# Expert-choice search of a hybrid diffusion step: step counts summed on VectorE, fp32r one-hot products for the ninth expert

## Chip, cores and metric

One core of a Trainium2 chip runs the whole kernel. The metric is device time in microseconds (us), the median of several executions. PE is TensorE's matmul queue, DVE is VectorE, ACT is ScalarE, POOL is GpSimd, SP issues most DMAs.

## The reference

One layer of a backbone: token mixing (projections, pooling, a bidirectional recurrence, gates) and then a mixture of 16 experts, for 128 context tokens and 1024 latent tokens of width 1024. The part that matters here is the mixture:

```python
def _expert_choice_moe(h, router_w, w1, w3, w2):
    bsz, n, d = h.shape
    cap = CAPACITY_FACTOR * n // N_EXPERTS
    aff = jax.nn.softmax(jnp.einsum('bnd,de->bne', h.astype(jnp.float32), router_w.astype(jnp.float32)), axis=-1)
    gate, idx = lax.top_k(jnp.swapaxes(aff, 1, 2), cap)
    xs = jax.vmap(lambda hb, ib: hb[ib])(h, idx)
    hid = jax.nn.silu(jnp.einsum('becd,edf->becf', xs, w1)) * jnp.einsum('becd,edf->becf', xs, w3)
    out = jnp.einsum('becf,efd->becd', hid, w2) * gate[..., None].astype(h.dtype)
    y = jax.vmap(lambda ib, ob: jnp.zeros((n, d), ob.dtype).at[ib.reshape(-1)].add(ob.reshape(-1, d)))(idx, out)
    return y.astype(h.dtype)
```

Each expert takes the 128 latent tokens (`cap`) with the largest affinity to it, and 16 of the context tokens. All of it is in float32.

## The kernel before

**Experts.** Up to about 811 us the kernel mixes tokens and routes; from there to the end it runs the experts, one after the other. An expert has 24 weight chunks of 1 MB. Each is loaded to `raw`, rounded to fp32r by ACT (`hi`, L1284), and DVE writes what rounding lost as bf16 (`lo`, L1290); the load of a later chunk is issued when `lo` is done with `raw`. PE multiplies high parts with `highs` (L1475) and low parts with `lows` (L1485). Four blocks `fb`, each for w1 and w3, and in each two pairs `q` of 128 columns make the hidden values; then the down projection makes `ot` (matrices `hh`, `hb`). After each pair `sums` adds the two halves of a PSUM accumulator: ACT copies one half (L1495), DVE adds the other (L1496). The accumulators come from a pool of three, so a pair starts when the sum of the pair three places before it is done. PE, DVE and ACT each work through their own queue in the order in which the code is written (`manual_schedule`); there is no planner.

**Search.** Which tokens an expert gets is found by a search for its threshold, three bits of the float at a time. `search(e0, e1)` is a generator for the n = e1 - e0 experts of a group: search(1, 5) runs in expert 0, search(5, 10) in experts 1 to 3, search(10, 16) in experts 4 to 6. Expert 0 needs no search of its own (its list is made before it). One `next` of it stands after `sums` of nearly every pair in expert 0 and after the first pair of each block in the later ones. The latent affinities `l8` lie as 128 partitions x 8 tiles x 16 experts. One step:

- DVE makes 8 candidate thresholds (`cand`) and compares all values with 7 of them: `msk`, 128 x (7 x 8 tiles x n), bf16 ones and zeros; plane 0 is all ones and is set once.
- PE multiplies `msk` with a matrix of ones, one product per tile, eight accumulated in one PSUM tile: the counts over partitions and tiles, on every partition.
- DVE keeps the candidates that enough tokens reach (`met`, L1387) and takes the largest (`th`, L1388).

After ten steps the search marks which values lie above the threshold and which equal it (`ge`), and PE numbers the marked tokens: one product with the triangle `upto`, seven with `ones` for the tiles before, eight more to count those above. From that DVE makes the places `slo`. `list_hot` and `list_make` (L1151, L1162 to L1167) turn an expert's places into its list, and `x_fetch` gathers the tokens from DRAM by it. In expert 0 this chain feeds expert 1 at once; later ones have an expert's time.

**Context tokens.** Their expert outputs are collected in `yps`, eight experts at a time. `finish_prompt(0)` (in expert 8, the ninth) transposes them, scales them by the gate (ACT, L1599), multiplies them with a one-hot matrix `oh` and adds them to `x2p`. `finish_prompt(1)` does so at the end.

Of the kernel before, what the change touches and what calls it, by code (L numbers as in the profile page):

```python
# [8 lines left out]
F32 = mybir.dt.float32  # L9
F32R = mybir.dt.float32r  # L10
BF16 = mybir.dt.bfloat16
I32 = mybir.dt.int32
U32 = mybir.dt.uint32
AF = mybir.ActivationFunctionType
OP = mybir.AluOpType
# [4 lines left out]
P = 128  # L20
D = 1024
# [28 lines left out]
def hybrid_step_kernel(ctx: ExitStack, tc: tile.TileContext, x_prompt, x_sample, state_lru, c, c_ctx,  # L50
# [14 lines left out]
    def tp_tile():  # L65
        return tpp.tile([P, 512], F32, name="tp")
# [1300 lines left out]

    l8 = lg[:, 1:, :]
    cand = ep.tile([P, 8, E], I32, name="cand")
    msk = ep.tile([P, 8, 8, E], BF16, name="msk")  # L1370
    V.memset(msk[:, 0], 1.0)

    def search(e0, e1):

# [2 lines left out]
        for b in range(10):  # L1377
            V.tensor_tensor(cand[:, :, es], bits[:, b, :, None].to_broadcast([P, 8, n]),
                            th.bitcast(I32)[:, None, es].to_broadcast([P, 8, n]), op=OP.bitwise_or)
            V.tensor_tensor(msk[:, 1:, :, es], l8_[:, None].to_broadcast([P, 7, 8, n]),  # L1380
                            cf[:, 1:, None, :].to_broadcast([P, 7, 8, n]), op=OP.is_ge)
            yield
            t = tp_tile()
            tv = t[:, :8 * n].rearrange("p (a b) -> p a b", a=8)
            for i in range(8):
                PE.matmul(tv, ones, msk[:, :, i, es], start=i == 0, stop=i == 7)
            V.scalar_tensor_tensor(met[:, :, es], tv, float(CAP), cf, op0=OP.is_ge, op1=OP.mult)  # L1387
            V.tensor_reduce(ths, met[:, :, es].rearrange("p a b -> p b a"), axis=AX.X, op=OP.max)  # L1388

        tb = ths[:, None, :].to_broadcast([P, 8, n])  # L1390
        V.tensor_tensor(ge[:, 0, :, es], l8_, tb, op=OP.is_gt)
        V.tensor_tensor(ge[:, 1, :, es], l8_, tb, op=OP.is_equal)
        yield
        t = tp_tile()[:, :16 * n].rearrange("p (m a b) -> p m a b", m=2, a=8)
        PE.matmul(t, upto, ge[:, :, :, es], start=True, stop=False)
        for i in range(1, 8):
            PE.matmul(t[:, :, i:], ones, ge[:, :, :8 - i, es], start=False, stop=False)
        for k in range(8):
            PE.matmul(t[:, 1], ones, ge[:, 0, k, None, es].to_broadcast([P, 8, n]), start=False, stop=k == 7)
        st = stg[:, :, :, es]  # L1400
        V.tensor_tensor(st, t, ge[:, :, :, es], op=OP.mult)
        V.scalar_tensor_tensor(st[:, 1], st[:, 1], float(CAP), st[:, 1], op0=OP.is_le, op1=OP.mult)
# [183 lines left out]

    def finish_prompt(g):

        oh = ep.tile([P, P], F32R, name="oh").bitcast(F32)
        V.tensor_scalar(oh, iof, pgf[:, g:g + 1], None, op0=OP.is_equal)  # L1590
        yield
        yp, pr = yps[g], []
        for h in range(2):
            t = tp_tile()
            for k in range(4):
                PE.transpose(t[:, k * P:(k + 1) * P], yp[:, 4 * h + k, :], ident)
            pr.append(ep.tile([P, 512], F32, name=f"pr{h}", tag=("h1", "ht")[h]) if g else
                      ew.tile([P, D], F32, name="rows", bufs=2)[:, :512])
            A.activation(pr[h], t, AF.Copy, scale=pgv[:, g:g + 1])  # L1599
            if g or h:  # L1600
                yield
        ts = []
        for h in range(2):
            hs = slice(h * 512, (h + 1) * 512)
            t = tp_tile()
            PE.matmul(t, oh, pr[h], start=True, stop=True)
            if g:
                yield
            V.tensor_tensor(x2p[:, hs], x2p[:, hs], t, op=OP.add)
            if g:  # L1610
                A.activation(last["junk"][:, :512], x2p[:, hs], AF.Square, accum_out=sqe[:, 3 + h:4 + h])
                yield


    find = search(1, 5)
# [201 lines left out]
```

## Time and profile before

| | us |
|---|---|
| median of 3 runs | 2096.61 (2096.43 to 2097.95) |
| profiled execution | 2096.98 |
| its span in the trace | 2095.2 |
| PE busy | 2036.8 (97%) |
| DVE busy | 1702.2 (81%) |
| ACT busy | 1365.5 (65%) |
| raw loads of expert weights | 380 of 1 MB, 7.1 us from issue to landing (median) |

Busy times are of one profiled execution. An engine's timeline says when an instruction starts, how long it takes, and in brackets how long the engine had been idle before it and what ended that. A busy share is an average over stages with different limits, so the table is only where the reading begins.

### The profile page before, as it was taken

The page shows a single profiled execution, that of the slowest core. Times are in us where ns is not written, and L with a number is a line of the kernel's source. Part 1 is how long each engine was busy: PE and PEld are TensorE (multiplying, and loading weights), DVE is VectorE, ACT ScalarE, POOL GpSimd, SP SyncE. Part 2 cuts the span into 40 slices and gives each one's busy share as a digit, 9 for nine tenths or more (in the row PEclk, how much of TensorE's full clock was granted, in tenths as well). Part 3 has the DMA queues.
Part 4 walks back from the last instruction along what each step waited for, and adds up shares of the span by engine and source line. Part 5 has one row for each costly group of instructions (what it writes and reads, how often), then busy time and mean ns, then how long its engine had stood idle before and what let it go on. Part 6 is the DMA issues. An engine that isn't in the chain of part 4 may idle for free.

```text
span 2095.2 us, 40732 instructions
## 1 busy us (share of the span) xinstructions
PE 2036.8 (97%) x17365; PEld 1961.8 (94%) x17365; DVE 1702.2 (81%) x1907; ACT 1365.5 (65%) x1437; POOL 188.0 (9%) x327
## 2 busy tenths in 40 slices
PE   7999999999999998999999999999999999999996
PEld 4899998999999886899999999999999999999996
DVE  7788988733145467999999999998899999999997
ACT  7477676322112236777877877877777877877875
POOL 0000001010012112010011010011010010010010
PEclk9999999999999998999999999999999999999998
DMA  8143444164755239999999999999999999999996
GB/s 273 57 121 113 120 128 120 43 192 152 202 163 188 101 132 323 311 328 323 345 333 329 348 324 333 351 345 322 339 337 327 349 341 322 352 341 327 349 342 252
DMA packets 303733, 544.72 MB, mean 260 GB/s; under 512 B 16235, under 2 KB 85563, under 8 KB 303550
## 3 DMA queue, kind: packets, MB, share of 16 engines
q1 hardware_dynamic: 284074, 478.56, 65.9%
q0 software_dynamic: 15872, 53.56, 8.7%
q10 hardware_dynamic: 3604, 9.98, 1.3%
q8 instruction: 136, 2.23, 0.4%
q14 instruction: 47, 0.39, 0.1%
HBM read 501.13 MB, written 40.93 MB: 259 GB/s over the span
## 4 chain that ended last, share of the span: by engine, by line
PE 88%; DVE 7%; ACT 2%; DMA 1%; issue 1%; SPq 0%; ACTq 0%; DVEq 0%; POOLq 0%
PE ac L1475 36%; PE ac L1485 17%; PE a L196 6%; PE a L197 6%; PE a L195 6%; PE a L778 5%; DVE lo L1290 2%; PE a L1002 2%; PE a L1004 2%; PE a L1003 2%; DMA xg<-hn_d,lgi 1%; PE tp L667 1%; PE tp L1413 1%; PE tp L1040 1%; PE tp L1506 1%
## 5 line engine op out<-in xcount | busy, mean ns | idle before, releaser
L1290 DVE TENSOR_TENSOR lo<-raw,hi 128x2048 bf16<-128x2048 f32 x384 | 872.0, 2284 | 0.0
L1284 ACT CAST hi<-raw 128x2048 fp32r<-128x2048 f32 x384 | 729.7, 1912 | 7.0 <-DMA raw<-in_exp_w_dram 4.1
L1475 PE MATMUL ac<-x,hi 128*128 128x288 f32 x4096 | 585.5, 298 | 0.0
L1475 PEld LDWEIGHTS ac<-x,hi 128*128 128x128 f32 x4096 | 548.6, 188 | 1.4 <-issue 1.1
L1485 PEld LDWEIGHTS <-lo 128*128 128x128 bf16 x6144 | 382.6, 98 | 17.1 <-DVE lo L1290 0.9
L1475 PE MATMUL ac<-hh,hi 128*128 128x288 f32 x2048 | 297.3, 298 | 0.0
L1485 PE MATMUL ac<-xb,lo 128*128 128x144 bf16 x4096 | 282.7, 226 | 0.0
L1495 ACT COPY bs<-ac 128x288 f32<-128x288 f32 x320 | 127.3, 398 | 237.5 <-PE ac L1475 125.7
L1475 PEld LDWEIGHTS ac<-hh,hi 128*128 128x128 f32 x2048 | 275.4, 188 | 0.0
L197 PE MATMUL a<-hn_hi,lo 128*128 128x384 f32 x624 | 210.5, 337 | 1.9 <-DVE lo L186 1.9
L195 PE MATMUL a<-hn_hi,hi 128*128 128x384 f32 x624 | 210.4, 337 | 0.0
L196 PE MATMUL a<-hn_lo,hi 128*128 128x384 f32 x624 | 210.2, 337 | 0.0
L1485 PE MATMUL ac<-hb,lo 128*128 128x144 bf16 x2048 | 147.1, 226 | 0.6 <-DVE lo L1290 0.6
L186 DVE TENSOR_TENSOR lo<-raw,hi 128x1024 fp32r<-128x1024 f32 (+1 forms) x77 | 88.3, 1164 | 64.4 <-ACT hi L185 64.4
L1496 DVE TENSOR_TENSOR h<-ac,bs 128x288 f32<-128x288 f32 x256 | 115.6, 451 | 22.5 <-ACT bs L1495 22.5
L197 PEld LDWEIGHTS a<-hn_hi,lo 128*128 128x128 f32 x624 | 117.7, 189 | 2.3 <-DVE lo L186 2.3
L195 PEld LDWEIGHTS a<-hn_hi,hi 128*128 128x128 f32 x624 | 118.0, 189 | 0.3
L196 PEld LDWEIGHTS a<-hn_lo,hi 128*128 128x128 f32 x624 | 117.9, 189 | 0.0
L185 ACT CAST hi<-raw 128x1024 fp32r<-128x1024 f32 (+1 forms) x77 | 75.8, 1001 | 47.3 <-PE a L196 36.7
L1761 POOL TENSOR_TENSOR yps<-ot,modc 128x128 f32<-128x128 f32 x15 | 35.5, 2370 | 706.5 <-DVE ot L1496 706.5
L1496 DVE TENSOR_TENSOR ot<-ac,bs 128x288 f32<-128x288 f32 x64 | 29.1, 457 | 52.8 <-ACT bs L1495 52.8
L701 ACT ACTIVATE sg<-a 128x1152 f32<-128x1152 f32 x16 | 18.1, 1134 | 78.4 <-PE a L197 78.3
(434 smaller groups left out, 2609.6 us busy)
## 6 DMA issues: line engine op xcount, KB each, us to landing
raw<-in_exp_w_dram SPq DMA_DIRECT2D x380, 1024.0 KB, 7.1
raw<-in_w_in_dram SPq DMA_DIRECT2D x28, 512.0 KB, 4.7
raw<-in_w_mod_dram SPq DMA_DIRECT2D x28, 512.0 KB, 5.5
araw<-in_w_mod_dram SPq DMA_DIRECT2D x18, 256.0 KB, 7.1
g_d<-sg ACTq DMA_DIRECT2D x8, 576.0 KB, 3.3
yh_d<-yh POOLq DMA_DIRECT2D x8, 576.0 KB, 3.1
yl_d<-yl POOLq DMA_DIRECT2D x8, 576.0 KB, 4.6
m_d<-sg POOLq DMA_DIRECT2D x8, 576.0 KB, 4.2
```

The source lines that it names most:

```text
L185: A.copy(h, raw)
L186: V.tensor_tensor(l, raw, h.bitcast(F32), op=OP.subtract)
L195: PE.matmul(out, whi, xhi, start=first, stop=False)
L196: PE.matmul(out, whi, xlo, start=False, stop=False)
L197: PE.matmul(out, wlo, xhi, start=False, stop=last)
L778: PE.matmul(a3[:, ch, :CH], w[:, k, :], y[:, k, cs], start=n == 0 and k == 0 and w is hi, stop=n == 1 and k == KD - 1 and w is ws[-1])
L1284: A.copy(hl[n][0], raw[n])
L1290: V.tensor_tensor(lo, r, hi.bitcast(F32), op=OP.subtract)
L1475: PE.matmul(a[:, r, :2 * S], w[0][:, k, c0 + r * P:c0 + (r + 1) * P], x2(kk), start=kk == first, stop=kk == last)
L1485: PE.matmul(a[:, r, S:2 * S], w[1][:, k, c0 + r * P:c0 + (r + 1) * P], xb(kk), start=False, stop=kk == last)
L1495: A.copy(b, a[:, :, S:2 * S])
L1496: V.tensor_tensor(dst, a[:, :, :S], b, op=OP.add)
```

## The change

In each step DVE sums the comparisons over the eight tiles into `cnt` (128 x 7 x n, bf16), and PE makes one product of it with `ones`; plane 0 of the counts is eight and is set once. At a search's end DVE makes running sums over the tiles in `pre`, a view of `msk`: the first tile's entry is zero for those above and the number of all above for those equal, and seven additions give the others; PE makes two products, with `upto` and with `ones`. In `finish_prompt(0)` the scaled rows are split in an fp32r part (ACT) and the rest (DVE), and each is multiplied with the one-hot matrix in fp32r: four products where there were two in float32.

```diff
@@ -1367,8 +1367,9 @@
 
     l8 = lg[:, 1:, :]
     cand = ep.tile([P, 8, E], I32, name="cand")
-    msk = ep.tile([P, 8, 8, E], BF16, name="msk")
-    V.memset(msk[:, 0], 1.0)
+    msk = ep.tile([P, 7, 8, E], BF16, name="msk")
+    cnt = ep.tile([P, 8, E], BF16, name="cnt")
+    V.memset(cnt[:, 0], 8.0)
 
     def search(e0, e1):
 
@@ -1377,26 +1378,31 @@
         for b in range(10):
             V.tensor_tensor(cand[:, :, es], bits[:, b, :, None].to_broadcast([P, 8, n]),
                             th.bitcast(I32)[:, None, es].to_broadcast([P, 8, n]), op=OP.bitwise_or)
-            V.tensor_tensor(msk[:, 1:, :, es], l8_[:, None].to_broadcast([P, 7, 8, n]),
+            V.tensor_tensor(msk[:, :, :, es], l8_[:, None].to_broadcast([P, 7, 8, n]),
                             cf[:, 1:, None, :].to_broadcast([P, 7, 8, n]), op=OP.is_ge)
+            with nc.allow_low_precision(reason="counts of at most eight"):
+                V.tensor_reduce(cnt[:, 1:, es], msk[:, :, :, es].rearrange("p a i e -> p a e i"), axis=AX.X, op=OP.add)
             yield
             t = tp_tile()
             tv = t[:, :8 * n].rearrange("p (a b) -> p a b", a=8)
-            for i in range(8):
-                PE.matmul(tv, ones, msk[:, :, i, es], start=i == 0, stop=i == 7)
+            PE.matmul(tv, ones, cnt[:, :, es], start=True, stop=True)
             V.scalar_tensor_tensor(met[:, :, es], tv, float(CAP), cf, op0=OP.is_ge, op1=OP.mult)
             V.tensor_reduce(ths, met[:, :, es].rearrange("p a b -> p b a"), axis=AX.X, op=OP.max)
 
         tb = ths[:, None, :].to_broadcast([P, 8, n])
         V.tensor_tensor(ge[:, 0, :, es], l8_, tb, op=OP.is_gt)
         V.tensor_tensor(ge[:, 1, :, es], l8_, tb, op=OP.is_equal)
+
+        pre = msk[:, :2]
+        V.memset(pre[:, 0, 0, es], 0.0)
+        with nc.allow_low_precision(reason="counts of at most eight"):
+            V.tensor_reduce(pre[:, 1, 0, es], ge[:, 0, :, es].rearrange("p i e -> p e i"), axis=AX.X, op=OP.add)
+        for i in range(1, 8):
+            V.tensor_tensor(pre[:, :, i, es], pre[:, :, i - 1, es], ge[:, :, i - 1, es], op=OP.add)
         yield
         t = tp_tile()[:, :16 * n].rearrange("p (m a b) -> p m a b", m=2, a=8)
         PE.matmul(t, upto, ge[:, :, :, es], start=True, stop=False)
-        for i in range(1, 8):
-            PE.matmul(t[:, :, i:], ones, ge[:, :, :8 - i, es], start=False, stop=False)
-        for k in range(8):
-            PE.matmul(t[:, 1], ones, ge[:, 0, k, None, es].to_broadcast([P, 8, n]), start=False, stop=k == 7)
+        PE.matmul(t, ones, pre[:, :, :, es], start=False, stop=True)
         st = stg[:, :, :, es]
         V.tensor_tensor(st, t, ge[:, :, :, es], op=OP.mult)
         V.scalar_tensor_tensor(st[:, 1], st[:, 1], float(CAP), st[:, 1], op0=OP.is_le, op1=OP.mult)
@@ -1586,30 +1592,46 @@
 
     def finish_prompt(g):
 
-        oh = ep.tile([P, P], F32R, name="oh").bitcast(F32)
+        oh = ep.tile([P, P], F32R, name="oh")
+        if g:
+            oh = oh.bitcast(F32)
         V.tensor_scalar(oh, iof, pgf[:, g:g + 1], None, op0=OP.is_equal)
         yield
         yp, pr = yps[g], []
+        if g == 0:
+
+            for h in range(2):
+                pr.append(ew.tile([P, 2, 512], F32R, name="rows", bufs=2))
+                t = tp_tile()
+                for k in range(4):
+                    PE.transpose(t[:, k * P:(k + 1) * P], yp[:, 4 * h + k, :], ident)
+                A.activation(pr[h][:, 0], t, AF.Copy, scale=pgv[:, g:g + 1])
+                V.scalar_tensor_tensor(pr[h][:, 1], t, pgv[:, g:g + 1], pr[h][:, 0].bitcast(F32), op0=OP.mult,
+                                       op1=OP.subtract)
+            yield
+            for h in range(2):
+                hs = slice(h * 512, (h + 1) * 512)
+                t = tp_tile()
+                for a in range(2):
+                    PE.matmul(t, oh, pr[h][:, a], start=a == 0, stop=a == 1)
+                V.tensor_tensor(x2p[:, hs], x2p[:, hs], t, op=OP.add)
+            yield
+            return
         for h in range(2):
             t = tp_tile()
             for k in range(4):
                 PE.transpose(t[:, k * P:(k + 1) * P], yp[:, 4 * h + k, :], ident)
-            pr.append(ep.tile([P, 512], F32, name=f"pr{h}", tag=("h1", "ht")[h]) if g else
-                      ew.tile([P, D], F32, name="rows", bufs=2)[:, :512])
+            pr.append(ep.tile([P, 512], F32, name=f"pr{h}", tag=("h1", "ht")[h]))
             A.activation(pr[h], t, AF.Copy, scale=pgv[:, g:g + 1])
-            if g or h:
-                yield
-        ts = []
+            yield
         for h in range(2):
             hs = slice(h * 512, (h + 1) * 512)
             t = tp_tile()
             PE.matmul(t, oh, pr[h], start=True, stop=True)
-            if g:
-                yield
+            yield
             V.tensor_tensor(x2p[:, hs], x2p[:, hs], t, op=OP.add)
-            if g:
-                A.activation(last["junk"][:, :512], x2p[:, hs], AF.Square, accum_out=sqe[:, 3 + h:4 + h])
-                yield
+            A.activation(last["junk"][:, :512], x2p[:, hs], AF.Square, accum_out=sqe[:, 3 + h:4 + h])
+            yield
 
 
     find = search(1, 5)
```

How it moves instructions, at three places. DVE in expert 0, third block, a search step between two low-part splits. Before:

```order
L1496 TENSOR_TENSOR h_7400<-ac,bs 128x288
L1387 SCALAR_TENSOR_TENSOR met<-tp,cand 128x8x4
L1388 TENSOR_REDUCE th<-met 128x4
L1378 TENSOR_TENSOR cand<-bits,th 128x8x4
L1380 TENSOR_TENSOR msk<-lg,cand 128x56x4
L1290 TENSOR_TENSOR lo<-raw,hi 128x2048
```

And now:

```order
L1502 TENSOR_TENSOR h_7360<-ac,bs 128x288
L1389 SCALAR_TENSOR_TENSOR met<-tp,cand 128x8x4
L1390 TENSOR_REDUCE th<-met 128x4
L1379 TENSOR_TENSOR cand<-bits,th 128x8x4
L1381 TENSOR_TENSOR msk<-lg,cand 128x56x4
L1384 TENSOR_REDUCE cnt<-msk 128x7x4
L1290 TENSOR_TENSOR lo<-raw,hi 128x2048
```

One reduction stands between the comparison and the next split; everything else keeps its place.

DVE in expert 0, fourth block, the end of search(1, 5). Before:

```order
L1388 TENSOR_REDUCE th<-met 128x4
L1391 TENSOR_TENSOR ge<-lg,th 128x8x4
L1392 TENSOR_TENSOR ge<-lg,th 128x8x4
L1290 TENSOR_TENSOR lo<-raw,hi 128x2048
L1496 TENSOR_TENSOR h_7518<-ac,bs 128x288
```

And now:

```order
L1390 TENSOR_REDUCE th<-met 128x4
L1393 TENSOR_TENSOR ge<-lg,th 128x8x4
L1394 TENSOR_TENSOR ge<-lg,th 128x8x4
L1397 MEMSET msk 128x4
L1399 TENSOR_REDUCE msk<-ge 128x4
L1401 TENSOR_TENSOR msk<-msk,ge 128x2x4 x7
L1290 TENSOR_TENSOR lo<-raw,hi 128x2048
L1502 TENSOR_TENSOR h_7466<-ac,bs 128x288
```

Nine operations are put between the marks and the next split.

PE in expert 0, a search step among the low products (weight loads stand as rows of their own). Before, the first two of eight such pairs:

```order
L1485 LDWEIGHTS lo
L1485 MATMUL ac<-xb,lo 128x144
L1386 LDWEIGHTS ones
L1386 MATMUL tp<-msk,ones 128x32
L1386 LDWEIGHTS ones
```

And now the whole step:

```order
L1491 LDWEIGHTS lo
L1491 MATMUL ac<-xb,lo 128x144
L1388 LDWEIGHTS ones
L1388 MATMUL tp<-cnt,ones 128x32
L1491 LDWEIGHTS lo
```

Seven of the eight pairs are gone; the one that is left stands at the same place and reads `cnt`.

## Rows read from the trace of the kernel before

**Rows 1.** The page's busy times: us, share of the span, instructions.
```profile
PE 2036.8 (97%) x17365; PEld 1961.8 (94%) x17365; DVE 1702.2 (81%) x1907; ACT 1365.5 (65%) x1437; POOL 188.0 (9%) x327
```

**Rows 2.** Windows of experts 0 and 1: length, busy PE, PEld, DVE, ACT, POOL, clock, DMA.
```profile
811.00:898.70 87.70, 82.26 (x884) 79.58 (x885) 82.98 (x105) 66.66 (x64) 4.08 (x2) 0.99 0.92 322
898.70:977.10 78.40, 78.40 (x818) 77.32 (x817) 74.61 (x74) 61.95 (x60) 7.38 (x4) 1.00 0.93 325
```

**Rows 3.** Timeline of PE, expert 0: start, duration, instruction, idle before and its releaser.
```profile
851.89 0.35 PE L1386 MATMUL tp<-msk,ones 128*128 128x32 bf16 x8 [0.61 <-DVE msk L1380]
...
888.31 1.09 PE L1413 MATMUL tp<-ident,xg 128*128 128x128 f32 x8 [1.62 <-DMA xg<-hn_d,lgi]
```

**Rows 4.** Timeline of DVE, expert 0.
```profile
851.74 2.29 DVE L1290 TENSOR_TENSOR lo<-raw,hi 128x2048 bf16<-128x2048 f32 x1
...
878.77 0.16 DVE L1164 COPY lc<-tp 128x5 f32<-128x5 f32 x1
878.96 0.16 DVE L1165 SCALAR_TENSOR_TENSOR lgi<-lc 128x1 int32<-128x1 f32 x1
...
892.96 1.36 DVE L1433 TENSOR_TENSOR x<-xf,x 128x1152 fp32r<-128x1152 f32 x1 [1.83 <-ACT x L1432]
```

**Rows 5.** Groups by line and shape, reductions: count, busy us, mean ns, idle before.
```profile
L1388 DVE TENSOR_REDUCE th<-met 128x6 f32<-128x48 f32 x10 | 2.4, 236 | 0.3
L1388 DVE TENSOR_REDUCE th<-met 128x4 f32<-128x32 f32 x10 | 2.1, 210 | 0.3
L1060 DVE TENSOR_REDUCE mx<-lg 128x1 f32<-128x16 f32 x2 | 0.3, 170 | 0.6 <-ACT lg L1056 0.6
L1060 DVE TENSOR_REDUCE mx<-lg 128x5 f32<-128x80 f32 x1 | 0.2, 238 | 0.3 <-ACT lg L1056 0.3
```

**Rows 6.** Timeline of PE, a search step in expert 1 and an end in expert 3.
```profile
928.69 0.40 PE L1386 MATMUL tp<-msk,ones 128*128 128x40 bf16 x8
928.93 1.16 PE L1485 MATMUL ac<-xb,lo 128*128 128x144 bf16 x16
...
1098.76 0.22 PE L1395 MATMUL tp<-ge,upto 128*128 128x80 bf16 x1
...
1099.26 1.16 PE L1485 MATMUL ac<-xb,lo 128*128 128x144 bf16 x16
```

**Rows 7.** Timelines of DVE and PE, where the down projection begins (experts 1, 3, 5).
```profile
949.67 0.45 DVE L1496 TENSOR_TENSOR h<-ac,bs 128x288 f32<-128x288 f32 x1
950.94 1.48 PE L1475 MATMUL ac<-hh,hi 128*128 128x288 f32 x10
...
1106.23 0.46 DVE L1496 TENSOR_TENSOR h<-ac,bs 128x288 f32<-128x288 f32 x1
1108.45 1.48 PE L1475 MATMUL ac<-hh,hi 128*128 128x288 f32 x10
...
1264.45 0.45 DVE L1496 TENSOR_TENSOR h<-ac,bs 128x288 f32<-128x288 f32 x1
1265.22 1.48 PE L1475 MATMUL ac<-hh,hi 128*128 128x288 f32 x10
```

**Rows 8.** Timeline of DVE, down projection of expert 1, first and last idle piece.
```profile
963.61 0.46 DVE L1496 TENSOR_TENSOR ot<-ac,bs 128x288 f32<-128x288 f32 x1 [0.65 <-ACT bs L1495]
...
977.73 0.46 DVE L1496 TENSOR_TENSOR ot<-ac,bs 128x288 f32<-128x288 f32 x1 [1.14 <-ACT bs L1495]
```

**Rows 9.** Timeline of PE, expert 8, and the group of L1609.
```profile
1460.23 4.47 PE L1475 MATMUL ac<-x,hi 128*128 128x288 f32 x32
1464.55 2.17 PE L1485 MATMUL ac<-xb,lo 128*128 128x144 bf16 x32
...
1486.58 2.10 PE L1475 MATMUL ac<-x,hi 128*128 128x288 f32 x14
...
1492.61 2.17 PE L1485 MATMUL ac<-xb,lo 128*128 128x144 bf16 x32
...
L1609 DVE TENSOR_TENSOR x2p<-x2p,tp 128x512 f32<-128x512 f32 x4 | 2.7, 684 | 0.5 <-PE tp L1606 0.5
```

## The prediction

> **What bounds the kernel now.** I read the page's busy times first, then the windows by expert, then the timelines of TensorE (PE) and VectorE (DVE) in the experts that hold a search. PE is busy for 97% of the span, DVE for 81% [rows 1]; by that alone, fewer products would mean less time. The windows split this. Expert 0 (811 to 898.7 us) takes 87.7 us and PE is busy for only 82.26 of them; expert 1 takes 78.4 us and PE has no idle time at all [rows 2]. So there are two regimes, and the search lies in both: search one (4 experts wide) runs in expert 0, search two (5 wide) in experts 1 to 3, search three (6 wide) in experts 4 to 6.
>
> In expert 0 PE stops and waits for the comparison of the search step itself: 0.61 us before the products at 851.89 [rows 3]. DVE on the other side runs its queue without a hole from 811 until 892.96, where the first idle time stands (1.83 us) [rows 4]. The queue there is, step after step: comparison, one low-part split of 2.29 us, accumulator sum, next comparison. The small operations that pick expert 1's tokens (lc, from 878.77) stand in the same queue; the gather of the tokens waits for them, and PE waits 1.62 us for the gather at 888.31 [rows 3]. So from 811 to 898 the time is DVE's queue, not PE's. In experts 1 to 6 PE sets the time, but DVE is busy for 74.61 of 78.4 us [rows 2], and all its idle time lies in the second half of an expert (the first piece after 903 is 0.65 us at 963.61, the last 1.14 us at 977.73) [rows 8]. Between these, DVE runs behind PE.
>
> **The change, part by part.**
>
> *The new reduction in each step.* Ten per search, 30 in all, 7 x 8 x n comparisons to 7 x n counts, in eights. No row shows this shape. Two rows bound it. The reduction of met (L1388), also in eights and with a stride, takes 210 ns for 4 groups and 236 for 6: 13 ns a group, 158 ns fixed [rows 5]. That gives 0.52, 0.61 and 0.70 us for 28, 35 and 42 groups. The unstrided reduction at L1060 takes 170 ns for 16 and 238 ns for 80 elements, 1.06 ns an element and 153 fixed [rows 5]: 0.39, 0.45 and 0.51 us. In the queue a dependent operation adds its duration and about 0.03 us (lc: 0.16 long, the next starts 0.19 later) [rows 4]. So a step costs DVE 0.42 to 0.55 us at 4 experts, 0.48 to 0.64 at 5, 0.54 to 0.73 at 6. L1388 is nearer in shape, but the data is bf16 at half the stride, so I take halfway: 0.485, 0.56 and 0.635.
>
> The Trainium skill, "VectorE: DVE Perf Modes", section "The perf-mode tier table", says that tensor_reduce has only a 1x form, and its rules for authors call it the slowest DVE operation, to be kept off a hot path. L1060 agrees with one element a cycle; L1388's 13 ns for eight, against 8.5, is dearer than that. By the page's rule the low ends hold and the sum below would be +5.2 us, by L1388 +11.6; the sign is the same.
>
> *The chain at a search's end.* One memset, one reduction and seven dependent additions of 2n elements. About 0.1, then 0.24 (L1388's 0.21 and 0.03), then 7 x 0.19 (lc's pace): 1.7 us. Ends: 1.4 at 0.15 each, 1.95 at 0.23.
>
> *Expert 0.* The first of ten reductions stands before the token parts, where DVE waits anyway: no cost. Nine and the chain go into the queue without a hole: 9 x 0.485 + 1.7 = 6.1 us (5.2 to 6.9). DVE never waits for the search product there (it has a 2.3 us split to do first), so the products removed give nothing back: PE only waits longer. lc, the gather and expert 1's start move by the same 6.1 us. What hides it: nothing, since PE's 1.62 us wait for the gather moves along.
>
> *Experts 1 to 6, PE.* Eight products take 0.24 us (928.69 to 928.93) [rows 6]; one of them is about 0.05, so 0.19 a step, 20 steps, 3.8 us. A search's end takes 0.50 us (1098.76 to 1099.26) [rows 6], two products 0.1: twice 0.4. Together 4.6 us less on PE, if DVE follows.
>
> *Experts 1 to 6, DVE.* Does it? An accumulator pair has three buffers. The second pair of the down projection (ninth matmul of hh) takes the buffer that the sum of the pair (fourth block, w3, first half) frees on DVE. Expert 1: the sum ends at 950.12, the ninth matmul starts at 950.94 + 8 x 0.135 = 952.0 (0.135: 32 of them in 4.32 us [rows 9]): DVE has 1.9 us in hand. Expert 5: 1264.90 against 1266.3, 1.4 us. Expert 3: 1106.69 against 1109.5, 2.8 us [rows 7]. DVE starts each expert in step with PE (the 1.14 us wait) and has no hole until there, so everything added comes off this reserve, and beyond it the expert ends that much later than it does now, whatever PE saves: PE's saving only lets it arrive earlier at the same wait. Experts 1, 2, 4 and 5 have four reductions each; I take 1.65 (mean of 1.4 and 1.9) for all four. n=5: 4 x 0.56 - 1.65 = 0.59, twice 1.2. n=6: 4 x 0.635 - 1.65 = 0.89, twice 1.8. Experts 3 and 6 have two reductions and the chain against 2.8: 1.12 + 1.7 - 2.8 = 0.0 and 1.27 + 1.7 - 2.8 = 0.2. Sum 3.2 us *longer*. Ends: 5.4 with the dear prices (0.9 twice, 1.27 twice, 0.4, 0.6); 0.8 with the cheap ones (0.27 twice, 0.5 twice, -0.4, -0.3). Behind the wait, DVE uses up its idle time in the down projection (about 3 us) and is in step again, so nothing is carried on.
>
> *Ninth expert.* 14 + 18 high products take 4.32 us without the one-hot products (1460.23 to 1464.55) and 6.03 with them (1486.58 to 1492.61) [rows 9]: 1.71 us for two fp32 products of 512 columns. Four fp32r ones at the pace of 288 columns in 0.135: 4 x 0.24 = 0.96. Saves 0.75 us on PE, which bounds there. The two DVE operations that it adds are of 512 columns, as L1609's addition (684 ns [rows 9]), 1.4 us in all. Expert 8 has no search, so they come off its reserve (at least 1.4 us as in expert 5, which has four steps of a search on top) and off nothing else: no cost; without that cover they would take back up to 1.4.
>
> **Sum.** 6.1 + 3.2 - 0.75 = +8.5 us on the profiled execution (2096.98 us, span 2095.2 of it): 2105.5. The median of the runs shown is 0.4 lower, so 2105.1. With the cheap ends 5.2 + 0.8 - 0.8 = +5.2 (2101.8), with the dear ones 6.9 + 5.4 - 0.7 = +11.6 (2108.2).
>
> **The rivals.**
>
> A: *the reserve holds* (no slower). If a step costs DVE under about 0.4 us, four of them stay within 1.65 us, PE keeps its 4.6 us in experts 1 to 6, and only expert 0 pays: 9 x 0.4 + 1.7 - 4.6 - 0.75 = 0 us, 2096.6; with 0.485 and a reserve that is larger than I read it, +0.8. For it: the low bound at n=4 is 0.42, just above. Against it: five and six wide the bound is 0.48 and 0.54.
>
> B: *expert 0 is PE's after all* (faster). If its added work hid in slack that the timeline doesn't show, 4.6 + 0.75 would come through: 2091.3. Against it: no hole in DVE's queue for 80 us, and PE's waits name the comparison.
>
> C: *the reduction is dearer than any row*: bf16 pairs at a stride cost twice the excess of L1388, 17.5 ns a group. Steps of 0.68, 0.80 and 0.92: expert 0 7.8, experts 1 to 6 2 x 1.55 + 2 x 2.0 + 0.5 + 0.7 = 8.3, less 0.75: +15.4, 2112.0. For it: why L1388 is dearer than L1060 no row tells, so it may grow with another shape. Against it: no reduction in the trace costs that much a group.
>
> **How the numbers follow.** Forecast 0.74, A 0.13, B 0.05, C 0.08. A measurement of this kernel tells about 0.2% (4.2 us) from no change, so slower means above 2100.8. The forecast's band lies above that, as does C: 0.82, less 0.02 for a forecast that falls short, 0.80. A is the same: 0.13 and those 0.02, less 0.01 for a step shorter still, 0.14. B and that 0.01 make faster 0.06. The range leaves out B and most of A below, and reaches C's figure above: 2099.5 to 2112.
>
> **What would show it.** In the changed profile: the reduction's row at 0.39 to 0.52 us (n=4) and 0.51 to 0.70 (n=6); expert 0 about 6 us longer, with PE waiting 0.9 us and more for cnt at most search steps and DVE still without a hole; in experts 1, 2, 4 and 5 PE waits of 1 to 2 us for a DVE sum, or at its place, right at the start of the down projection, where there are none now; expert 8 shorter by 0.75. I am wrong if experts 1 to 6 get shorter by 0.6 to 0.8 us each (A), if the reduction lies outside its bounds, or if PE's waits in expert 0 don't grow.

## The result and the profile after

| | before | after |
|---|---|---|
| median, us | 2097.28 (2096.43 to 2099.80) | 2116.14 (2113.59 to 2118.76) |
| profiled execution, us | 2096.98 | 2114.91 |
| its span, us | 2095.2 | 2113.1 |

The ratio is 1.0083, with an interval of 1.0071 to 1.0095: 15 to 20 us slower, where 8.5 were forecast and 2112.0 was the upper end. The sign was right, the size was not.

The page's busy times after, to be set against [rows 1]: PE has 252 products fewer and hardly any busy time less, DVE has 25 us more.

```profile
PE 2036.4 (96%) x17113; PEld 1957.2 (93%) x17113; DVE 1727.3 (82%) x1966; ACT 1360.2 (64%) x1437; POOL 189.8 (9%) x327
```

To see where the time went, take PE's timeline and note when each expert's first high product starts. The differences are the experts' lengths in us; they are used for all kernels below. (Start is that of expert 0 from the start of the span. Experts 9 to 14 are alike, so one stands for them.)

| | start | 0 | 1 | 2 | 3 | 4 | 5 | 6 | 7 | 8 | 9 |
|---|---|---|---|---|---|---|---|---|---|---|---|
| before | 810.92 | 87.79 | 78.39 | 78.63 | 78.88 | 78.29 | 78.49 | 78.73 | 78.57 | 80.29 | 77.69 |
| after | 811.75 | 97.36 | 79.84 | 80.27 | 79.41 | 80.04 | 80.55 | 79.57 | 78.57 | 79.50 | 77.69 |
| difference | +0.83 | +9.57 | +1.45 | +1.64 | +0.53 | +1.75 | +2.06 | +0.84 | 0 | -0.79 | 0 |

Expert 0 takes 9.57 us more, experts 1 to 6 together 8.27 more, expert 8 takes 0.79 less. With the 0.83 at the start that is 17.88 of the span's 17.9. The start lies ahead of all that was changed, and varies between 809.7 and 813.8 in the traces of this case: no effect of the change.

**The reduction's price.** The groups by line and shape after, DVE, L1384 and the comparison L1381 (count, busy us, mean ns, idle before):

```profile
L1384 DVE TENSOR_REDUCE cnt<-msk 128x42 bf16<-128x336 bf16 x10 | 7.9, 792 | 0.3
L1384 DVE TENSOR_REDUCE cnt<-msk 128x35 bf16<-128x280 bf16 x10 | 6.9, 688 | 0.3
...
L1384 DVE TENSOR_REDUCE cnt<-msk 128x28 bf16<-128x224 bf16 x10 | 5.6, 560 | 0.3
...
L1381 DVE TENSOR_TENSOR msk<-lg,cand 128x224 bf16<-128x224 f32 x10 | 4.0, 401 | 0.3
```

From 28 to 42 groups of eight the reduction grows by 232 ns: 16.6 ns a group, where the bounds taken from [rows 5] were 8.5 and 13. All three shapes lie above the dear bound (0.52, 0.61 and 0.70 us).

**Expert 0.** DVE's timeline after, one search step, then the end of the search, then the first operation of the chain to the gather (start, duration):

```profile
855.84 0.40 DVE L1381 TENSOR_TENSOR msk<-lg,cand 128x224 bf16<-128x224 f32 x1
856.27 0.56 DVE L1384 TENSOR_REDUCE cnt<-msk 128x28 bf16<-128x224 bf16 x1
856.75 2.28 DVE L1290 TENSOR_TENSOR lo<-raw,hi 128x2048 bf16<-128x2048 f32 x1
...
869.55 0.19 DVE L1394 TENSOR_TENSOR ge<-lg,th 128x32 bf16<-128x32 f32 x1
869.67 0.21 DVE L1399 TENSOR_REDUCE msk<-ge 128x4 bf16<-128x32 bf16 x1
869.69 0.06 DVE L1397 MEMSET msk<- 128x4 bf16 x1
869.92 1.41 DVE L1401 TENSOR_TENSOR msk<-msk,ge 128x8 bf16<-128x8 bf16 x7
871.24 2.28 DVE L1290 TENSOR_TENSOR lo<-raw,hi 128x2048 bf16<-128x2048 f32 x1
...
886.53 0.16 DVE L1164 COPY lc<-tp 128x5 f32<-128x5 f32 x1
```

Before, the comparison of such a step stands here, and the split behind it at 851.74 [rows 4]:

```profile
851.43 0.40 DVE L1380 TENSOR_TENSOR msk<-lg,cand 128x224 bf16<-128x224 f32 x1
```

A split may start 0.91 us after the comparison instead of 0.31, so a step adds 0.60. The chain adds 1.6 (869.55 to 871.24, against 0.10 without it). lc stands at 886.53 where it stood at 878.77 [rows 4]: 7.76, less the 0.83 of the start, is 6.93 us. The queue still has no hole: after its first operations the first idle time in the expert is 3.54 us ahead of 902.44. PE's waits in expert 0 after, in total (us, times, longest):

```profile
PE tp L1388 <- DVE cnt L1384: 9.3, 7, 2.1
PE tp L1419 <- DMA xg<-hn_d,lgi: 2.7, 1, 2.7
PE tp L1404 <- DVE msk L1397: 1.5, 1, 1.5
PE tp L1405 <- DVE msk L1401: 1.4, 1, 1.4
```

The other 2.64 us of the 9.57 lie behind lc. PE's timeline and its granted clock (in a window's row the third number from the right, as a share of full speed) show them:

```profile
897.12 1.81 PE L1419 MATMUL tp<-ident,xg 128*128 128x128 f32 x8 [2.75 <-DMA xg<-hn_d,lgi]
898.58 3.34 PE L1481 MATMUL ac<-hh,hi 128*128 128x288 f32 x16
901.77 2.17 PE L1491 MATMUL ac<-hb,lo 128*128 128x144 bf16 x32
```

```profile
897.00:902.00 5.00, 4.88 (x28) 4.80 (x29) 1.90 (x1) 3.62 (x4) 0.00 (x0) 0.66 1.04 387
```

From lc to the transposes it is 10.59 us, against 9.54 before (878.77 to 888.31, [rows 3, 4]): the gather takes 1.05 more. And after PE's wait of 2.75 us the eight transposes and 16 high products take 4.65 us (897.12 to 901.77) instead of 3.05 (888.31 to 891.36): 1.60 more. The granted clock there is 0.66. An estimate from this: if it was 1.2 GHz for 0.68 of the 5 us and 2.4 for the rest, that mean comes out, and 3.4 us at half speed are 1.7 us lost.

**Experts 1 to 6.** The timelines of DVE and PE where the down projection of expert 1 begins, to be read with [rows 7], and PE's groups from 948 to 1400 us (last: idle time before, and who ended it):

```profile
963.22 0.46 DVE L1502 TENSOR_TENSOR h<-ac,bs 128x288 f32<-128x288 f32 x1
...
961.79 0.69 PE L1481 MATMUL ac<-hh,hi 128*128 128x288 f32 x4
963.73 0.53 PE L1481 MATMUL ac<-hh,hi 128*128 128x288 f32 x2 [1.24 <-DVE h L1502]
```

```profile
L1481 PE MATMUL ac<-hh,hi 128*128 128x288 f32 x768 | 113.3, 299 | 5.8 <-DVE h L1502 5.5
```

The sum ends at 963.68 and releases the ninth matmul of `hh` 0.05 us later: the very pair of instructions that the prediction named. The same wait of 1.24 us stands in experts 2, 4 and 5, and one of 0.25 and 0.28 in 3 and 6. Before, that group has no idle time (937 to 1363 us):

```profile
L1475 PE MATMUL ac<-hh,hi 128*128 128x288 f32 x736 | 106.6, 298 | 0.0
```

These waits are not the whole loss, and the ninth matmul is not the only place where PE stops. In the fourth block of expert 1, for one, a set of 32 high products takes 4.56 us from its start to the next instruction's (4.32 in [rows 9]); the view counts no idle time there.

```profile
952.49 4.72 PE L1481 MATMUL ac<-x,hi 128*128 128x288 f32 x32
957.05 2.17 PE L1491 MATMUL ac<-xb,lo 128*128 128x144 bf16 x32
```

Set against best, a kernel below in which PE doesn't stop, experts 1 to 6 are 12.7 us longer. By the starts of the matmuls about 7.1 of that lie at the ninth matmul, the rest in shorter stops at accumulators of the third and fourth block. Those should add nothing to the time: DVE has no hole in expert 1 between 909.74 and 976.98, so its queue sets when the ninth matmul starts, and PE, late already, only waits less there.

**Expert 8.** PE's timeline after:

```profile
1505.23 2.10 PE L1481 MATMUL ac<-x,hi 128*128 128x288 f32 x14
1507.17 1.09 PE L1616 MATMUL tp<-rows,oh 128*128 128x512 f32 x4
1508.10 2.54 PE L1481 MATMUL ac<-x,hi 128*128 128x288 f32 x18
1510.48 2.17 PE L1491 MATMUL ac<-xb,lo 128*128 128x144 bf16 x32
```

1505.23 to 1510.48 is 5.25 us, where it was 6.03 [rows 9]: 0.78 less.

### The profile page after: what moved, and what is told of

The parts are those of the page before. It is cut to its first block, busy times and chain, and to the rows that moved or that the text cites. A ratio compares the mean times of both kernels' runs of the same rounds, so it can differ in the third digit from the quotient of the medians.

```text
span 2113.1 us, 40286 instructions
## 1 busy us (share of the span) xinstructions
PE 2036.4 (96%) x17113; PEld 1957.2 (93%) x17113; DVE 1727.3 (82%) x1966; ACT 1360.2 (64%) x1437; POOL 189.8 (9%) x327
## 5 line engine op out<-in xcount | busy, mean ns | idle before, releaser
L1694 ACT ACTIVATE h<-h 128x576 f32<-128x576 f32 x64 | 43.7, 683 | 46.8 <-DVE h L1502 46.8
```

Source lines behind the costliest of these rows:

```text
L1694: A.activation(h, h, AF.Silu)
```

## The experiments

The theory: a step costs DVE 0.60 to 0.82 us because the reduction reads bf16 values at a stride; in expert 0 all of it is on the path, in experts 1 to 6 all beyond the lead that DVE has where the down projection begins. Rivals: the loss lies in PE's new order or waits themselves, or in the one search and not the other; the reduction is dear whatever its layout; the lower clock is a cause and not a follower.

**One search each way.** Two kernels undo half of the change: search one by products again, or searches two and three.

```diff
+        new, cs = e0 > 1, slice(e0 - 5, e1 - 5)     # e0_products; late_products has e0 == 1, slice(e0 - 1, e1 - 1)
...
-            PE.matmul(tv, ones, cnt[:, :, es], start=True, stop=True)
+            if new:
+                PE.matmul(tv, ones, cnt[:, :, cs], start=True, stop=True)
+            else:
+                for i in range(8):
+                    PE.matmul(tv, ones, msk[:, :, i, es], start=i == 0, stop=i == 7)
```

> Search one (expert 0) as before the change, with eight products a step and sixteen at its end; the later searches and the ninth expert as changed. Theory (VectorE's queue pays in both places): expert 0 is back at about 87.7 us and its clock dip is gone, experts 1 to 6 stay 8.3 us longer than before, expert 8 stays 0.8 shorter: 7 to 8 us above the kernel before, about 10 below the changed one. Rival (only expert 0 pays, the rest is something that follows from it): at or below the kernel before.

> The other half: search one as changed, the searches in experts 1 to 6 as before the change. Theory: experts 1 to 6 are back at 78.3 to 78.9 us each without waits of TensorE for VectorE's sums; expert 0 pays 9 x 0.60 + 1.6 = 7.0 us in VectorE's queue and up to 2.6 in a longer gather and a lower clock behind it; less 0.8: 6 to 9 us above the kernel before. Rival (later experts pay whatever form expert 0 has): 15 or more above. With the run beside it, the two extra times should add up to that of the change, 17 to 18 us, plus the 0.8 counted twice.

Measured: late_products 2107.47 us (ratio 1.0044, 1.0027 to 1.0060), e0_products 2111.21 (1.0067, 1.0050 to 1.0084). The lengths:

| | 0 | 1 | 2 | 3 | 4 | 5 | 6 | 7 | 8 | 9 |
|---|---|---|---|---|---|---|---|---|---|---|
| late_products | 97.32 | 78.43 | 78.64 | 78.89 | 78.40 | 78.59 | 78.81 | 78.64 | 79.59 | 77.77 |
| e0_products | 88.42 | 79.97 | 80.43 | 79.53 | 80.86 | 80.67 | 79.70 | 78.95 | 79.88 | 78.08 |

late_products is 9.2 us above the kernel before by the ratio, just over the 6 to 9 that were expected; experts 9 to 14 at 77.77 instead of 77.69 are a part of that. So the two losses are apart: without sums in searches two and three experts 1 to 6 are as before, and without them in search one expert 0 is nearly so. But e0_products is 14 us above the kernel before where 7 to 8 were expected, and slower in experts that no search touches: expert 9 takes 78.08 us instead of 77.69. Its tiles had other sizes (eight planes of `msk`, `cnt` 11 wide, a small tile halved to make room), so the next two runs separate that.

**The same with the tiles of the changed kernel, and the tiles alone.** e0_prod2 keeps seven planes and feeds the plane of ones by a product of its own; places takes the changed kernel's work with the tile sizes of e0_products.

```diff
+            if old:           # e0_prod2, search one
+                PE.matmul(tv[:, 0], ones, cnt[:, 0, es], start=True, stop=True)
+                for i in range(8):
+                    PE.matmul(tv[:, 1:], ones, msk[:, :, i, es], start=i == 0, stop=i == 7)
```

```diff
-    msk = ep.tile([P, 7, 8, E], BF16, name="msk")     # places
-    cnt = ep.tile([P, 8, E], BF16, name="cnt")
+    msk = ep.tile([P, 8, 8, E], BF16, name="msk")
+    cnt = ep.tile([P, 8, 11], BF16, name="cnt")
-    sqe = ep.tile([P, 16], F32, name="sqe")
+    sqe = ep.tile([P, 8], F32, name="sqe")
```

> Search one by products again (nine a step, the ninth for the constant plane), the rest as changed, and now every tile of exactly the changed kernel's size. In the run with other tile sizes the experts without a search took 78.08 us each instead of 77.69, all of it in high products (4.35 us for 32 instead of 4.32). Theory (that pace came with the places of the tiles, not with the search): experts from 9 on at 77.69 again, expert 0 at 87.5 to 88.5, experts 1 to 6 as in the changed kernel: 7 to 8.5 us above the kernel before. Rival (products in expert 0 slow what follows): 78.08 and 13 above again.

> The changed kernel with the same work everywhere, but with the tile sizes of the kernel of the first study that kept products in search one: eight comparison planes instead of seven, counts 11 columns wide instead of 16, the squares 8 wide instead of 16. Theory 1 (the place of tiles in SBUF sets the pace of the high products): 32 high products take 4.35 us instead of 4.32 from expert 0 on, experts 9 to 14 take 77.95 to 78.1 instead of 77.69 us, and the time is 4 to 6 us above the changed kernel's, 2119 to 2122. Theory 2 (the slower pace there came from the products of search one or its order): the pace stays 4.32, experts 9 to 14 take 77.69, and the time is that of the changed kernel, about 2116.

e0_prod2: 2107.58 us (1.0036, 1.0022 to 1.0049); expert 0 takes 87.56, experts 1 to 6 take 79.82, 80.27, 79.41, 80.03, 80.59 and 79.57, as after, and expert 9 takes 77.69 again. places: 2119.52 (1.0102, 1.0086 to 1.0119); expert 9 takes 78.08. PE's timeline in expert 10, of the changed kernel and of places: 32 high products from 1648.97 to 1653.28 and from 1649.02 to 1653.37.

```profile
1648.97 4.47 PE L1481 MATMUL ac<-x,hi 128*128 128x288 f32 x32
1653.28 2.17 PE L1491 MATMUL ac<-xb,lo 128*128 128x144 bf16 x32
```

```profile
1649.02 4.51 PE L1483 MATMUL ac<-x,hi 128*128 128x288 f32 x32
1653.37 2.17 PE L1493 MATMUL ac<-xb,lo 128*128 128x144 bf16 x32
```

Same products, same queue, other sizes of three tiles and so other places in SBUF: 4.35 us for 32 instead of 4.31. An expert has twelve such sets: 0.48 us by these rounded starts, 0.39 by the lengths. It is no part of the change's loss, since expert 9 takes 77.69 both before and after; which tile it is, and why it matters, was not tried. Two things in e0_prod2's profiled time are not of the search: its span begins late (expert 0 at 813.31), and it is 103.10 us from the last expert's start to the end, 100.0 to 100.7 elsewhere. By the lengths its loss is that of experts 1 to 6, +8.28, less expert 8's 0.79.

**The stride.** Two kernels let the reduction read contiguous values. contig writes the comparison with the eight tiles innermost, so its writes get the stride; turned first copies the affinities in that order once per search, so that nothing has a stride.

```diff
-    msk = ep.tile([P, 7, 8, E], BF16, name="msk")     # contig
+    msk = ep.tile([P, 7, E, 8], BF16, name="msk")
-            V.tensor_tensor(msk[:, :, :, es], l8_[:, None].to_broadcast([P, 7, 8, n]),
+            V.tensor_tensor(msk[:, :, es].rearrange("p a e i -> p a i e"), l8_[:, None].to_broadcast([P, 7, 8, n]),
```

```diff
+        if flip:     # turned
+            V.tensor_copy(l8t[:, es], l8_.rearrange("p i e -> p e i"))
...
+            if flip:
+                V.tensor_tensor(mskt[:, :, es], l8t[:, None, es].to_broadcast([P, 7, n, 8]),
+                                cf[:, 1:, :, None].to_broadcast([P, 7, n, 8]), op=OP.is_ge)
```

> The changed kernel with the comparisons laid out so that the eight tiles of an expert lie side by side: the reduction reads them in a row instead of at a stride of 32 bytes, the comparison writes at a stride. Theory 1 (the stride makes the reduction dear, 16.6 ns for eight): reduction at 0.39, 0.45 and 0.51 us, the comparison unchanged; expert 0 loses 9 x 0.17 = 1.5 us less, experts 1 to 6 20 x 0.2 + 10 x 0.28 = up to 6 less in VectorE's queue: 5 to 8 us below the changed kernel. Theory 2 (a reduction of this shape costs 16 ns for eight in any layout): reduction at 0.56 to 0.79 as now, same time or slower by what the strided writes add.

> The changed kernel with the affinities of a search copied once so that an expert's eight tiles lie side by side; comparison and reduction then read and write in a row. Theory (strides of bf16 make both dear): comparison 0.40, 0.45 and 0.51 us, reduction 0.39, 0.445 and 0.50; a step adds 0.43, 0.40 and 0.53 us to VectorE's queue instead of 0.60, 0.77 and 0.88; expert 0 1.5 us shorter than in the changed kernel, experts 1 to 6, whose reserve of 1.4 to 1.9 us (2.6 and 2.8 with a chain) then nearly holds, 0.5 us above the kernel before in all instead of 8.3: about 9 us below the changed kernel. Rival (the reserve isn't what decides, the longer step is): 1.5 + 20 x 0.3 = 6 or less below, with waits left in all six experts.

contig: 2137.78 us (1.0193, 1.0176 to 1.0210). turned: 2106.95 (1.0036, 1.0023 to 1.0049). The groups of DVE, first contig, then turned:

```profile
L1381 DVE TENSOR_TENSOR msk<-lg,cand 128x336 bf16<-128x336 f32 x10 | 17.0, 1697 | 0.3
...
L1381 DVE TENSOR_TENSOR msk<-lg,cand 128x224 bf16<-128x224 f32 x10 | 11.3, 1131 | 0.3
L1384 DVE TENSOR_REDUCE cnt<-msk 128x42 bf16<-128x336 bf16 x10 | 5.0, 502 | 0.3
...
L1384 DVE TENSOR_REDUCE cnt<-msk 128x28 bf16<-128x224 bf16 x10 | 3.9, 389 | 0.3
```

```profile
L1394 DVE TENSOR_REDUCE cnt<-msk 128x42 bf16<-128x336 bf16 x10 | 5.0, 503 | 0.3
...
L1387 DVE TENSOR_TENSOR msk<-stg,cand 128x224 bf16<-128x224 f32 x10 | 4.2, 422 | 0.3
L1394 DVE TENSOR_REDUCE cnt<-msk 128x28 bf16<-128x224 bf16 x10 | 3.9, 389 | 0.3
```

The stride is the price: 389 ns contiguous, 560 with it, and 389 is the cheap bound of the prediction. Moved to the write it costs more (1131 instead of 401), and contig loses everywhere: its expectation held the comparison unchanged and gave 5 to 8 us less than the changed kernel, and it takes 21.6 more. In turned the lengths are 96.13, 78.45, 78.79, 78.68, 79.03, 79.39 and 78.98: experts 1 to 3 as before, 4 to 6 still longer by 0.74, 0.90 and 0.25, in all +1.9. A step now adds 0.41 us to DVE's queue five wide and 0.54 six wide; four of them are 1.6 and 2.2 us, against the lead of 1.65 that the prediction took. So most of the loss is gone, but not all: 0.5 us was expected to be left in experts 1 to 6, and PE still waits 0.25 us and more in each of them. PE's group, 948 to 1400, turned:

```profile
L1504 PE MATMUL ac<-hh,hi 128*128 128x288 f32 x768 | 113.0, 299 | 3.9 <-DVE h L1525 3.9
```

**The place of the work.** move leaves the work of the changed kernel as it is, and runs two of an expert's four steps between the two sums of each half of the down projection, where DVE has idle time [rows 8]. before_move does the same to the kernel before.

```diff
-                    if (e == 0 and (fb, w, q) not in SKIP) or (e and w == q == 0):
+                    if (e == 0 and (fb, w, q) not in SKIP) or (e and w == q == 0 and fb % 2 == 0):
...
                             sums(aa.pop(q), ot[:, 4 * dh + 2 * q:4 * dh + 2 * q + 2])
+                            if e and q == 0:
+                                next(find, None)
```

> The changed kernel, every operation as it is, but two of the four steps in each of experts 1 to 6 are put between the two sums of each half of the down projection, where VectorE has idle time; blocks one and three keep theirs. Theory (the wait at the start of the down projection comes from the work between an expert's start and that sum, not from the work in all): no waits of TensorE there; experts 1 to 6 together 0 to 3 us shorter than in the kernel before, instead of 8.3 longer, bounded by VectorE, which then has 78 us of work in 78: 8 to 11 us below the changed kernel. Rival (the added work counts wherever it stands): same time as the changed kernel within 2 us.

> The kernel before with two of the four search steps of an expert (experts 1 to 6) moved between the two sums of each half of the down projection, as in the moved kernel; counts still by products. Theory 1 (the moved place is worth something only because the added reductions fill VectorE's lead; without them nothing waits there): experts 1 to 6 keep 78.3 to 78.9 us, since PE had no idle time there and does the same products, and the time is 2096 to 2100, no change against the kernel before. Theory 2 (the place itself gains, and the gain of the best kernel is not due to fewer products): experts 1 to 6 take 77.8 to 78.0, as in the moved kernel, 3 to 4.5 us less in all.

move: 2104.23 us (1.0025, 1.0016 to 1.0034); experts 1 to 6 take 77.79, 77.82, 78.15, 77.77, 77.89 and 78.65, 3.3 us less than before instead of 8.3 more. before_move: 2097.97 (0.9998, 0.9989 to 1.0008), with lengths of 78.41, 78.64, 78.89, 78.30, 78.50 and 78.74, as before. DVE's timeline of move, a step in the down projection, and PE's group, 948 to 1400:

```profile
971.71 0.46 DVE L1502 TENSOR_TENSOR ot<-ac,bs 128x288 f32<-128x288 f32 x1 [0.68 <-ACT bs L1501]
...
973.43 0.72 DVE L1384 TENSOR_REDUCE cnt<-msk 128x35 bf16<-128x280 bf16 x1
974.05 0.46 DVE L1502 TENSOR_TENSOR ot<-ac,bs 128x288 f32<-128x288 f32 x1
```

```profile
L1481 PE MATMUL ac<-hh,hi 128*128 128x288 f32 x768 | 111.3, 298 | 0.0
```

The same reductions at the same price, and PE doesn't wait for these sums at all: the loss in experts 1 to 6 was the place. The time is some 12 us below the changed kernel's, a little more than the 8 to 11 expected. The move alone gains nothing, so the 3.3 us are the products that are gone.

**The clock.** fill gives PE 36 products, whose result nothing reads, ahead of the transposes that wait for the gather.

```diff
+                if e == 0 and n == XC:
+                    t = tp_tile()
+                    for k in range(36):
+                        PE.matmul(t[:, :S], ones, xb[:, k % KD, :], start=k == 0, stop=k == 35)
```

> The changed kernel with 36 idle products (bf16, 144 columns, 2.2 us in all, result not used) put before the transposes of expert 1's tokens in expert 0, where TensorE waits 2.75 us for their gather and ran at a granted clock of 0.66 for 5 us behind it. Theory (the wait lets the clock fall): granted clock 1.00 behind the gather, the stretch from the transposes to the next high products 1.6 us shorter, so 1 to 2 us below the changed kernel. Rival (the low clock comes from the many waits before, or from elsewhere): clock still at 0.6 to 0.7 there, same time.

2115.42 us (1.0081, 1.0064 to 1.0098); by the time alone no different from the changed kernel. The trace shows more: PE's timeline and the window from 898.7.

```profile
896.57 2.42 PE L1777 MATMUL tp<-xb,ones 128*128 128x144 bf16 x36
898.83 1.04 PE L1419 MATMUL tp<-ident,xg 128*128 128x128 f32 x8
899.62 2.36 PE L1481 MATMUL ac<-hh,hi 128*128 128x288 f32 x16
901.83 2.17 PE L1491 MATMUL ac<-hb,lo 128*128 128x144 bf16 x32
```

```profile
898.70:903.70 5.00, 5.00 (x59) 4.93 (x57) 2.70 (x3) 4.24 (x5) 0.00 (x0) 1.00 1.04 387
```

With PE kept busy the clock is 1.00 there, and transposes and products take 3.00 us instead of 4.65. Expert 0 gets 1.03 shorter (96.33), not 1.65, because lc comes 75.32 us after its start instead of 74.78. The trace shows why. In this execution the clock is low twice before, from 859 to 862 us and behind PE's two waits at the end of the search (1.50 and 1.39 us). There 18 high products take 4.00 us instead of 2.47 (871.40 to 873.87 in the changed kernel), and DVE waits for the sum behind them. A window, PE and DVE of fill:

```profile
873.00:876.00 3.00, 3.00 (x15) 3.00 (x14) 2.93 (x6) 0.68 (x1) 0.00 (x0) 0.50 0.44 98
...
872.52 4.16 PE L1481 MATMUL ac<-x,hi 128*128 128x288 f32 x18
876.52 2.17 PE L1491 MATMUL ac<-xb,lo 128*128 128x144 bf16 x32
...
878.22 0.46 DVE L1502 TENSOR_TENSOR h<-ac,bs 128x288 f32<-128x288 f32 x1 [0.42 <-ACT bs L1501]
```

Its span begins 1.1 us later, which hides the rest of the gain. So it is shown that the 1.60 us are the price of the lower clock. That PE's longer wait for the gather brings the low clock is not shown: move and places have no idle products, and their clock behind the gather is 1.00 too. Over all traces it is low there behind waits of 1.94 (turned), 2.50 (contig), 2.69 (late_products) and 2.75 us (after), and not behind 1.38 to 2.13 in the six kernels without sums in search one, nor behind 1.76 (places) and 2.33 (move): the length of this wait alone doesn't decide. Where it is not low behind the gather, it is low earlier: from 865 to 880 us its mean is 0.89 in places, move and fill (in turned and contig too), and 1.00 in after and late_products. So each of the seven kernels that sum in search one has a stretch of low clock in the later part of expert 0, and the six others have none from 826 us on; what decides its place stays open.

**The ninth expert alone, and the parts that pay together.** f32r_only changes the ninth expert's products in the kernel before, and nothing else. best has search one by products (as e0_prod2), searches two and three as turned and in the places of move, and the ninth expert's products as changed.

```diff
+        old, flip = e0 == 1, e0 > 1     # best: products in search one, turned sums in the others
```

> The kernel before with the ninth expert's products alone changed. Theory 1 (the parts add): expert 8 takes 79.5 instead of 80.29 us, every other expert as before; 0.8 us less, 0.04%, which the time alone can hardly tell (2096 to 2098). Theory 2 (two more VectorE operations of 512 columns cost something of their own): expert 8 stays at 80.3 or is longer.

> Search one by products as before the change, searches two and three with the turned comparison and two of four steps in the down projection, the ninth expert's products as changed. Theory: expert 0 as before; VectorE has 76.6 to 77.2 us of work in experts 1 to 6 against TensorE's 77.8, so TensorE keeps its 0.57 to 0.8 us in each: 4.4 in all, and 0.8 in expert 8: 5 us below the kernel before (0.25%). Rival (sums in the down projection come late and stop TensorE there): 0 to 3 below.

f32r_only: 2098.46 us (1.0001, 0.9992 to 1.0011); expert 8 takes 79.50, experts 1 to 7 and 9 to 14 are as before. best: 2093.05 against 2099.47 for the kernel before, measured beside it (0.9971, 0.9960 to 0.9982), faster than both kernels; lengths 87.78, 77.78, 77.82, 77.89, 77.77, 77.80, 77.86, 78.57, 79.50, 77.69: 4.5 us less in experts 1 to 6, 0.8 in expert 8, none lost in expert 0. PE's group, 948 to 1400:

```profile
L1504 PE MATMUL ac<-hh,hi 128*128 128x288 f32 x768 | 111.3, 298 | 0.0
```

## Why the prediction was right in its structure and short in its size

*The step that failed* is the first: "No row shows this shape. Two rows bound it." They did not. The rows were bounds only if a stride on bf16 costs no more than one on fp32, and nothing in the trace said so. The reduction measured 0.56, 0.69 and 0.79 us, each above its dear end (0.52, 0.61 and 0.70), which the prediction had named as a sign of being wrong. For a step I took 0.485, 0.56 and 0.635 us; it cost 0.60, 0.77 and 0.82. Rival C had the right mechanism (17.5 ns a group, measured 16.6) and a chance of 0.08: too little, for a price that no row held. That C's 8.3 us for experts 1 to 6 is what was measured is in part luck: its steps (0.80 and 0.92) were too dear, and the lead that it shared with the forecast too large.

The Trainium skill, "Vector Engine (DVE) Microarchitecture Reference", section "5.2 Measured stream behaviour on trn2", has a table, measured on 4-byte words in an operation with two sources, by which a stream whose elements don't come in adjacent pairs takes about 1.7 to 2.5 ns a column instead of 1.05. The slope here is 2.07 ns an element with the stride (232 ns for 112) and 1.01 without (502 less 389), which agrees, though it is bf16 in a reduction; by it the high price would have been the likely one.

*Expert 0's queue.* "9 x 0.485 + 1.7 = 6.1" became 9 x 0.60 + 1.6 = 7.0, measured 6.93. The chain was right to 0.1 us, the form of the sum was right, the reductions short by 1.0 us in all.

*What hides it: "nothing, since PE's 1.62 us wait for the gather moves along".* It moved along and grew to 2.75. I priced the shift and not what follows a longer wait: 1.60 us of lower clock (with the clock at 1.00, in fill, the same work takes 3.00 us and not 4.65; why the clock falls there stays open). And the gather itself took 9.5 us from issue to landing instead of 8.4. This is no scatter: it takes 9.3 to 9.9 in all seven kernels that sum in search one, and 8.2 to 9.0 in all six that don't. What it runs into when it is issued later was not tried; loads of `raw` run beside it in both.

*Experts 1 to 6.* The wait that was named came, in the four experts that were named, as did the two small ones. "4 x 0.56 - 1.65" was short by the price again: a step adds 0.77 us five wide and 0.82 six wide (the reduction, 0.03 and a small rest), the chain 1.6. With these and the reserves as they were taken: 2 x 1.43 + 2 x 1.63 + 0.34 + 0.44 = 6.9, measured 8.27. The other 1.4 us are the reserve, which was taken a little too large: what the experts lost leaves 1.2 to 1.65 us of it in experts 1, 2, 4 and 5 instead of 1.65, and 2.4 and 2.6 instead of 2.8 in 6 and 3. It is also why a small error in price came through fourfold: the term is a difference of near equals, 0.59 forecast where 1.45 and 1.64 were measured. That PE's saving is worth nothing behind that wait was right too; move and best show it come through as soon as the wait is gone (4.5 of the 4.6 us counted).

*Ninth expert.* 0.75 forecast, 0.79 measured, and f32r_only gives the same alone.

*The sum* of the profiled execution: 6.9 + 1.05 + 1.6 in expert 0, 8.3 in experts 1 to 6, -0.8 in expert 8, and 0.8 of the start that is no effect. Of the 9.4 us that the forecast lacked, about 4.5 are the reduction's price (0.8 in expert 0, 3.7 in experts 1 to 6), 1.4 the reserve, 2.65 the longer gather and the lower clock behind it, 0.8 the start. The range was too narrow for the first two and had no place for the third.

## What to carry to other kernels

When a step is put into a queue that another engine is about to wait for, its worth is its cost less the lead at that place, and that small difference multiplies any error in price: look for the lead first, and for a place in the queue with idle time, since the same work moved there cost nothing. A price for a shape that no row shows needs an end that allows for its layout, above all a stride on two-byte data. And a wait that grows can cost more than its length, where the engine's clock is lower behind it.

## What the runs showed of the hardware

- Summing bf16 values 32 bytes apart takes 2.07 ns an element, contiguous ones 1.01; a comparison that writes bf16 values 16 bytes apart takes 1131, 1448 and 1697 ns for 224, 280 and 336 of them, 5.05 ns an element between the ends, and 401, 580 and 508 as the changed kernel writes them (why five wide is dearer than six was not tried).
- PE's granted clock has a mean of 0.66 over 5 us behind a wait of 2.75 us, and the work there takes 4.65 us instead of the 3.00 at 1.00. It is low in the later part of expert 0 in all seven kernels whose search one sums on DVE, and in none of the six others; behind which wait differs from kernel to kernel.
- The same 32 fp32r products take 4.31 or 4.35 us when three tiles have other sizes, and so other places in SBUF (after and places): 0.39 us in each of experts 9 to 14, a source of small differences between kernels that do the same work.
